# The second FFN's first two blocks on x times A, with the norm's factor and the part of B applied afterwards

## Chip, cores and metric

The kernel runs on one core of one Trainium2 chip. The metric is the device time of one execution in microseconds (us), taken as the median of several runs. Engines are named as in the profile: PE is TensorE's matmuls and PEld its weight loads, DVE is VectorE, ACT is ScalarE, POOL is GpSimd, and SP is SyncE, which issues the DMAs.

## What is computed

The reference is a model block of two layers followed by a second hybrid block. The change touches one place, the feed-forward network (FFN) of the second layer, on the 256 latent tokens (width 1024):

```python
def rmsnorm(x, g):
    y = x * lax.rsqrt(jnp.mean(x * x, axis=-1, keepdims=True) + EPS)
    return y * g

def modulate(x, g, shift, scale):
    return rmsnorm(x, g) * (1 + scale) + shift
...
# FFN: h = modulate(x, ...); u = h @ w_up (1024 -> 2 * 2816);
# a 3x3 depthwise convolution over a grid of 4 rows x 64 tokens, plus a bias;
# hidden = first half * silu(second half); x += gate * (hidden @ w_down)
```

In the kernel's terms h = (x · r) · A + B. A = g · (1 + scale) and B = shift have one value per feature. r is the norm's factor, one value per token.

## The kernel before

Activations lie feature-major: 128 features on the partitions, tokens along the free axis, 8 groups k of 128 features. `xT` is the residual stream in float32; the latent tokens are its columns 256 to 511. Every matmul operand is a pair of a float16 part and a bfloat16 rest (`whi`, `wlo` for weights, `hh`, `hl` for h), and a product takes three passes, whi·hh, whi·hl and wlo·hh (`proj_fm`, line 332).

Layer 1's mixer ends in `ssd`. Its last generator, `out(3, factor)`, multiplies the products `so` by a factor (DVE) and adds them to `xT` (`add_residual`, DVE). Then `ffn(1, ...)` runs:

- `norm_h` (line 378) calls `rstd_bc` (line 354). ACT squares each of the 8 groups and DVE adds them up (`sq`). A matmul with ones gives the sum per token (`ssq`). DVE makes the reciprocal root in eleven small instructions, spreads it on a diagonal (`dg`), and a matmul brings it to all partitions in PSUM (`rbc`, one buffer of the pool `nb`). Then for each k: DVE forms `nt` = x·A·r, ACT rounds it with B to `hh`, DVE forms the rest `hl`.
- The up projection has 22 blocks. Block i has 256 columns of `w_up`, as two channels of 128 (c = 0, 1). For each channel PE makes 8 × 3 matmuls of 256 tokens into a PSUM tile `up` (pool `mm`, 7 buffers). `conv` then has ACT write u = up · w4 + bias, and DVE adds the 8 other taps, each one `scalar_tensor_tensor` (line 1005, recorded at the helper's line 303) that reads `up` from PSUM and `u` from SBUF. ACT takes the silu (`sg`), POOL multiplies (`sg` by u), ACT and POOL split the result into `hidh` and `hidl`.
- The weights of blocks 0 and 1 (`first_up`) are loaded and split during the mixer. Those of block 2 are split by ACT (`whi`) and DVE (`wlo`), those of later blocks by ACT and POOL (`wlo`, 128x2048). The split weights have three buffers, so `whi` of block i waits for PE to be through with block i − 3.
- The down projection (`dn`) follows, with `before_norm` and early weights of the next stage between its steps.

The order on each engine's queue is settled when the program is built: an instruction that is ready goes ahead of an earlier one that still waits, and among ready ones the earlier one in the program goes first. `reuse_waits="tile"` means that a pool's new memory waits for the tiles that lay there before.

Of the kernel before, what the change touches and what calls it, by code (L numbers as in the profile page):

```python
# [10 lines left out]
F32 = mybir.dt.float32  # L11
F16 = mybir.dt.float16
BF16 = mybir.dt.bfloat16
I32 = mybir.dt.int32
U32 = mybir.dt.uint32
AF = mybir.ActivationFunctionType
ALU = mybir.AluOpType
# [231 lines left out]
class Program:  # L249
# [723 lines left out]
    def ffn(self, l, streams):  # L973
        I, V = self.I, self.V
        both = len(streams) == 2
        n, t0 = (512, 0) if both else (256, 256)
        lat = n - 256
        fcb = self.pp("fcb").rearrange("p (l c) -> p l c", l=2)[:, l]
        h = self.h
        if both:  # L980

            self.norm_stream(l, 1, 1)
            first = []
            for i in range(3):
                w = self.get_w(I["w_up"][l, i], 8, 256, self.G)
                first.append((w, [self.mm("up") for _ in range(2)]))
                for c in range(2):
                    self.proj_fm(first[i][1][c][:, :256], w, c * 128, 128, h, 0, 256)
        else:
            self.norm_h(self.xT, t0, n, self.segs(l, 1, streams), h)  # L990

        def conv(u, ps, c):
            w = lambda j: fcw[:, c, j:j + 1]
            self.act(u[:, :n], ps[:, :n], AF.Identity, bias=fcb[:, c:c + 1], scale=w(4))
            if both:
                self.stt(u[:, 1:256], ps[:, 0:255], w(3), u[:, 1:256], ALU.mult, ALU.add)
                self.stt(u[:, 0:255], ps[:, 1:256], w(5), u[:, 0:255], ALU.mult, ALU.add)
            ug, pg = [a[:, lat:lat + 256].rearrange("p (r c) -> p r c", r=4) for a in (u, ps)]
            for dy in (-1, 0, 1):
                for dx in (-1, 0, 1):  # L1000
                    if dy == 0 and dx == 0:
                        continue
                    r0, r1, c0, c1 = max(0, -dy), 4 - max(0, dy), max(0, -dx), 64 - max(0, dx)
                    o = ug[:, r0:r1, c0:c1]
                    self.stt(o, pg[:, r0 + dy:r1 + dy, c0 + dx:c1 + dx], w(3 * dy + dx + 4), o, ALU.mult, ALU.add)

        with ExitStack() as ph:
            fp = self.pool("fp", 1, None, ph)
            f2 = self.pool("f2", 3, None, ph)
            stage = self.pool("stage", 1 if both else 3, None, ph)  # L1010
            fcw = fp.tile([128, 44, 9], F32, name="fcw")
            self.nc.sync.dma_start(fcw, I["fcw"][l].rearrange("p (c j) -> p c j", c=44))
            hid = self.pair(fp, "hid", [128, 22, n])
            if both:
                ms, mp = self.pool("ms", 3, None, ph), self.pool("mp", 3, None, ph)
                up = True
                mods = chain.from_iterable(self.mod_steps(1, r, eng=lambda: self.G if up else None, pool=ms, parts=mp,
                                                          halves=True) for r in range(6))
            for i in range(22):
                begun = both and i < 3  # L1020
                if begun:
                    w, pss = first[i]
                elif not both and i < 2:
                    w = self.first_up[i]
                else:
                    w = self.get_w(I["w_up"][l, i], 8, 256, self.G if both or i > 2 else None, (None, stage)[i % 2])
                us = []
                for c in range(2):
                    ps = pss[c] if begun else self.mm("up")
                    a = 256 if begun else 0  # L1030
                    self.proj_fm(ps[:, a:n], w, c * 128, 128, h, a, n)
                    u = f2.tile([128, n], F32, tag=f"u{c}", name="u")
                    conv(u, ps, 22 * c + i)
                    us.append(u)
                sg = f2.tile([128, n], F32, tag="sg", name="sg")
                self.act(sg[:, :n], us[1][:, :n], AF.Silu)
                self.tt(sg[:, :n], sg[:, :n], us[0][:, :n], ALU.mult, eng=self.G)
                self.split(hid[0][:, i], hid[1][:, i], sg[:, :n], eng=self.G)
                if both:
                    next(mods)  # L1040

            def down(k, ws, a, b):
                ps = self.mm("dn")
                for j, w in enumerate(ws):
                    self.proj_fm(ps[:, a:b], w, 0, 128, hid, a, b, nk=11, h0=11 * j, first=j == 0, last=j == 1)
                    for _ in range(3 - j if both else 0):
                        next(mods, None)
                return ps

            def weights(k, j, parts=None):  # L1050
                return self.get_w(I["w_dn"][l, 2 * k + j], 11, 128, self.G if not both and k < 2 else None, (None, stage)[j], parts)

            up = False
            if not both:
                self.ahead()
            for k in range(6 if both else 8):
                self.add_residual(down(k, [weights(k, j) for j in range(2)], 0, n), l, 5, k, streams, t0)
                if not both:
                    self.before_norm(k)
                    if k >= 4 and k < 4 + 3:  # L1060
                        for i in (0, 1):
                            self.first_mg.append(self.get_w(I["w2_m"][2 * (k - 4) + i], 8, 128, self.G, stage, self.nx, 2048, 1024))
            if both:

                ws = [[weights(k, j, fp if (k, j) == (7, 1) else None) for j in range(2)] for k in (6, 7)]
                for s, a, b in streams:
                    for k in (6, 7):
                        ps = down(k, ws[k - 6], a, b)
                        self.add_residual(ps[:, a:b], l, 5, k, ((s, 0, 256),), a)
                    if s == 0:  # L1070
                        self.norm_stream(1, 0, 0)


    def layer1_mixer(self):
        h, I = self.h, self.I
        self.fu_stack = self.ctx.enter_context(ExitStack())
        with ExitStack() as ph:
            self.fu = self.pool("fu", 2, None, self.fu_stack)
            sp = self.pool("sp", 1, None, ph)
            s2 = self.pool("s2", 2, None, ph)  # L1080

            y = self.pair(sp, "ys", [128, 8, 256])
            self.ssd(sp, s2, h, y)
            self.dbg("ys", y[0])
        self.dbg("xmid1", self.xT[:, :, 256:512])

    def ssd(self, sp, s2, h, y):
# [198 lines left out]
        def heads(g, D):  # L1286
# [3 lines left out]
            for j in range(4):  # L1290
# [41 lines left out]
                                 start=True, stop=True)  # L1332
                self.tt(yt[:, j], yt[:, j], Y[:, :256], ALU.add)
                self.tt(yt[:, j], yt[:, j], D["sz"][:, j], ALU.mult)
                sq = s2.tile([128, 256], F32, tag="ssq", name="ssq", bufs=3)
                self.act(sq, yt[:, j], AF.Square)
                if j:
                    self.tt(sq, sq, sums, ALU.add)
# [663 lines left out]
```

## Time and profile before

| what | us |
|---|---|
| median of 3 runs (range) | 1651.38 (1649.72 to 1652.54) |
| the profiled execution | 1646.42 |
| its span | 1644.6 |
| PE busy in the span | 1563.6 (95%) |
| DVE busy | 1212.3 (74%) |
| ACT busy | 847.9 (52%) |
| POOL busy | 444.8 (27%) |

The span is the profiled execution between its first and last recorded instruction; positions such as 1075.31 are us from its start. Consecutive instructions of one engine overlap in the records, so the spacing of a run of them (its length divided by their count) is what one costs its engine, and it is less than one's recorded duration. A DVE or POOL instruction that is held up after it has been issued appears with a longer duration, not with idle time ahead of it.

### The profile page before, as it was taken

To read this page: it belongs to the slowest core of one execution; us is meant where nothing else is said; L and a number is where in the kernel's file an instruction comes from. 1 tells how busy PE (TensorE), PEld (TensorE's weight loads), DVE (VectorE), ACT (ScalarE), POOL (GpSimd) and SP (SyncE) were. 2 spreads that over 40 slices of the span, in tenths; PEclk is the share of its full clock that TensorE was granted. 3 is DMA by queue.
4 is the path that set the end of the run, shared out by engine and by line. 5 is a ranking of instruction groups with operands and counts; after the bars stand their busy time and mean duration, and the time that the engine had idled before them with its cause. 6 is when DMAs were issued, how large, how long until landed. Compare 5 with 4: busy or idle time off the path is not lost.

```text
span 1644.6 us, 31809 instructions
## 1 busy us (share of the span) xinstructions
PE 1563.6 (95%) x12978; PEld 1083.6 (66%) x12978; DVE 1212.3 (74%) x2637; ACT 847.9 (52%) x1390; POOL 444.8 (27%) x264
## 2 busy tenths in 40 slices
PE   6999999889999999998999999699998999999998
PEld 3565875467444444475566667488887887778877
DVE  6888856777877796557878898799977885366734
ACT  4746434334555445435555665356564644566542
POOL 0000000224878740000000000259934312431250
PEclk9999999989999999999999999799999999999999
DMA  9222135752444437532222343335454343433651
GB/s 392 89 103 79 54 126 208 258 183 80 157 149 146 138 122 254 177 120 77 103 78 95 112 141 125 124 121 199 137 194 166 141 167 111 146 116 125 228 168 52
DMA packets 41187, 236.77 MB, mean 144 GB/s; under 512 B 4689, under 2 KB 5457, under 8 KB 21201
## 3 DMA queue, kind: packets, MB, share of 16 engines
q1 hardware_dynamic: 41040, 234.74, 40.6%
q8 instruction: 102, 1.67, 0.4%
q14 instruction: 45, 0.36, 0.1%
HBM read 233.68 MB, written 1.05 MB: 143 GB/s over the span
## 4 chain that ended last, share of the span: by engine, by line
PE 81%; DVE 8%; ACT 4%; DMA 3%; issue 3%; POOL 1%; ACTq 0%; SPq 0%; DVEq 0%; POOLq 0%
PE up L332 19%; PE dn L332 9%; PE sx L332 5%; PE fm L332 4%; PE mg L332 4%; PE br L332 3%; PE mqk L332 2%; PE tm L339 2%; ACT whi L306 2%; PE so L332 2%; DVE wlo L294 2%; PE mod L505 2%; PE sz L332 2%; DVE u L303 2%; PE sc L1664 2%
## 5 line engine op out<-in xcount | busy, mean ns | idle before, releaser
L332 PEld LDWEIGHTS <-whi 128*128 128x128 f16 (+2 forms) x5240 | 511.5, 99 | 253.3 <-issue 38.1
L294 POOL TENSOR_TENSOR wlo<-st,whi 128x2048 bf16<-128x2048 f32 (+2 forms) x101 | 311.7, 3097 | 935.5 <-ACT whi L306 934.8
L306 ACT ACTIVATE whi<-st 128x2048 f16<-128x2048 f32 (+3 forms) x242 | 369.1, 1536 | 253.3 <-PE dn L332 46.6
L332 PEld LDWEIGHTS <-wlo 128*128 128x128 bf16 (+2 forms) x2620 | 258.9, 99 | 127.4 <-issue 13.6
L294 DVE TENSOR_TENSOR wlo<-st,whi 128x2048 bf16<-128x2048 f32 (+4 forms) x141 | 279.0, 1988 | 83.8 <-ACT whi L306 82.1
L303 DVE SCALAR_TENSOR_TENSOR u<-up,fcw,u 128x189 f32<-128x189 f32 (+3 forms) x792 | 297.3, 431 | 49.4 <-ACT u L306 41.5
L332 PE MATMUL up<-hh,whi 128*128 128x256 f16 (+1 forms) x752 | 238.2, 319 | 4.4 <-ACT hh L306 4.1
L332 PE MATMUL up<-hl,whi 128*128 128x256 bf16 (+1 forms) x752 | 238.1, 317 | 2.0 <-DVE hl L303 1.9
L332 PE MATMUL up<-hh,wlo 128*128 128x256 f16 (+1 forms) x752 | 237.7, 317 | 0.0
L332 PE MATMUL dn<-hidh,wlo 128*128 128x256 f16 (+1 forms) x396 | 122.2, 310 | 2.3 <-DVE wlo L294 2.3
L332 PE MATMUL dn<-hidh,whi 128*128 128x256 f16 (+1 forms) x396 | 122.3, 311 | 1.8 <-ACT whi L306 1.8
L332 PE MATMUL dn<-hidl,whi 128*128 128x256 bf16 (+1 forms) x396 | 122.5, 310 | 0.0
L306 ACT ACTIVATE u<-up,ppt,fcw 128x512 f32<-128x512 f32 (+1 forms) x88 | 58.1, 660 | 47.9 <-PE up L332 47.9
L332 PE MATMUL fm<-hh,whi 128*128 128x256 f16 x288 | 78.5, 273 | 0.5 <-DVE xc L303 0.5
L332 PE MATMUL fm<-hh,wlo 128*128 128x256 f16 x288 | 78.6, 273 | 0.0
L332 PE MATMUL fm<-hl,whi 128*128 128x256 bf16 x288 | 78.5, 273 | 0.0
L332 PE MATMUL mg<-hh,wlo 128*128 128x256 f16 x256 | 71.0, 277 | 3.6 <-POOL wlo L294 3.6
L332 PE MATMUL mg<-hl,whi 128*128 128x256 bf16 x256 | 71.0, 278 | 1.2 <-DVE hl L303 1.2
L332 PE MATMUL mg<-hh,whi 128*128 128x256 f16 x256 | 70.7, 277 | 0.9 <-ACT mgt L306 0.9
L339 PEld LDWEIGHTS <-hh 128*128 128x128 f16 x640 | 61.5, 99 | 8.8 <-issue 1.1
L298 POOL TENSOR_SCALAR E<-E,rs 128x128 f32<-128x128 f32 (+1 forms) x48 | 37.1, 786 | 107.3 <-DVE rs L1675 47.9
L294 POOL TENSOR_TENSOR sg<-sg,u 128x512 f32<-128x512 f32 (+1 forms) x44 | 44.2, 1004 | 45.6 <-ACT sg L306 45.3
(539 smaller groups left out, 3050.8 us busy)
## 6 DMA issues: line engine op xcount, KB each, us to landing
st<-in_w_up_dram SPq DMA_DIRECT2D x44, 1024.0 KB, 4.8
st<-in_w_dram SPq DMA_DIRECT2D x25, 1024.0 KB, 4.9
st<-in_mod_w_dram SPq DMA_DIRECT2D x48, 512.0 KB, 4.7
st<-in_w_dn_dram SPq DMA_DIRECT2D x32, 704.0 KB, 4.1
st<-in_ssd_w_dram SPq DMA_DIRECT2D x20, 1024.0 KB, 4.9
st<-in_mod_w_dram SPq DMA_DIRECT2D x16, 1024.0 KB, 6.4
st<-in_w_m_dram SPq DMA_DIRECT2D x32, 512.0 KB, 4.3
st<-in_even_w_dram SPq DMA_DIRECT2D x14, 1024.0 KB, 5.0
```

Source lines behind the costliest of these rows:

```text
L294: (eng or self.V).tensor_tensor(o, a, b, op=op)
L298: (eng or self.V).tensor_scalar(o, a, s1, None, op0=op0)
L303: self.V.scalar_tensor_tensor(o, a, s, b, op0=op0, op1=op1)
L306: self.S.activation(o, i, func, **kw)
L332: self.T.matmul(ps, w[a][:, k, c0:c0 + cw], h[b][:, h0 + k, t0:t1], start=first and k == 0 and i == 0, stop=last and k == nk - 1 and i == 2)
L339: self.T.matmul(ps, h[b][:, k, t0:t0 + 128], w[a][:, k, c0:c0 + cw], start=k == 0 and i == 0, stop=k == nk - 1 and i == 2)
L505: T.matmul(ps[32 * j:32 * j + 32, :256], c[:, 2 * b + k], w[:, 0 if halves else k, 256 * j:256 * j + 256], start=b == k == i == 0, stop=b ...
L1664: T.matmul(ps[:, a:b], q[r, tb * 128:tb * 128 + 128], k[r, 0:b - a], start=True, stop=False)
```

## The change

Ahead of `norm_h`, x·A (without r and B) is split into the unused columns 256 to 511 of `h`, for all 8 groups. `rstd_bc` is called by itself. Blocks 0 and 1 are multiplied with x·A into four PSUM tiles. B, split and padded to 32 columns, is multiplied with the same weights into a PSUM tile `uB` (four strips of 32 partitions, two k in each), copied to SBUF as a row and summed over its partitions by a matmul with ones; this gives one value per output feature, `ub`. The factor r is copied from PSUM to SBUF (`rb`). When blocks 0 and 1 come up in the loop, DVE multiplies each of their four products by `rb` into an SBUF tile (tag `sg`, 3 buffers), ACT adds `ub` to it in place, and `conv` reads that SBUF tile where it read PSUM before. Blocks 2 to 21 use the normed h as before. The two tiles of B take 1 KB per partition, which the tag `ssq` gives back (3 buffers become 2).

```diff
         else:
-            self.norm_h(self.xT, t0, n, self.segs(l, 1, streams), h)
+            (_, _, A, B), = self.segs(l, 1, streams)
+            for k in range(8):
+                self.split(h[0][:, k, 256:512], h[1][:, k, 256:512], self.xT[:, k, 256:512], scale=A(k))
+            pb = self.rstd_bc(self.xT, t0, n)
+            hB = [self.fb.tile([128, 8, 32], dt, name=m) for m, dt in (("hBh", F16), ("hBl", BF16))]
+            bB = self.modc[l][:, 3, 1]
+            for t in hB:
+                self.G.memset(t, 0.0)
+            self.act(hB[0][:, :, 0], bB)
+            self.tt(hB[1][:, :, 0], bB, hB[0][:, :, 0], ALU.subtract)
+            first = []
+            for w in self.first_up:
+                pss = [self.mm("up") for _ in range(2)]
+                for c in range(2):
+                    self.proj_fm(pss[c][:, :256], w, c * 128, 128, h, 256, 512)
+                ps = self.mm("uB")
+                for k in range(8):
+                    j = k % 4
+                    for i, (a, b) in enumerate(PASSES):
+                        self.T.matmul(ps[32 * j:32 * j + 32, :256], hB[b][:, k], w[a][:, k],
+                                      start=k < 4 and i == 0, stop=k >= 4 and i == 2)
+                row = self.cols.tile([128, 256], F32, tag="mrow", name="mrow", bufs=1)
+                self.act(row, ps[:, :256])
+                for c in range(2):
+                    self.T.matmul(ps[:, 256 + c:257 + c], row[:, c * 128:c * 128 + 128], self.ones[:, 0:1], start=True, stop=True)
+                ub = self.cols.tile([128, 2], F32, tag="ub", name="ub")
+                self.act(ub, ps[:, 256:258])
+                first.append((pss, ub))
+            rb = self.nrm.tile([128, 512], F32, tag="s2", name="rb")
+            self.act(rb[:, :n], pb[:, :n])
+            self.norm_h(self.xT, t0, n, self.segs(l, 1, streams), h, pb)
...
-                    w = self.first_up[i]
+                    pss, ub = first[i]
...
-                    ps = pss[c] if begun else self.mm("up")
-                    a = 256 if begun else 0
-                    self.proj_fm(ps[:, a:n], w, c * 128, 128, h, a, n)
+                    if not both and i < 2:
+                        ps = f2.tile([128, n], F32, tag="sg", name="up")
+                        self.tt(ps, pss[c][:, :n], rb[:, :n], ALU.mult)
+                        self.act(ps, ps, AF.Identity, bias=ub[:, c:c + 1])
+                    else:
+                        ps = pss[c] if begun else self.mm("up")
+                        a = 256 if begun else 0
+                        self.proj_fm(ps[:, a:n], w, c * 128, 128, h, a, n)
...
-            self.fu = self.pool("fu", 2, None, self.fu_stack)
+            self.fu, self.fb = self.pool("fu", 2, None, self.fu_stack), self.pool("fb", 1, None, self.fu_stack)
...
-                sq = s2.tile([128, 256], F32, tag="ssq", name="ssq", bufs=3)
+                sq = s2.tile([128, 256], F32, tag="ssq", name="ssq")
```

## Rows read from the trace of the kernel before

**Rows 1.** Stretches: length, busy (count) of PE, PEld, DVE, ACT, POOL, clock, DMA, GB/s.
```profile
1050.00:1054.50 4.50, 1.36 (x13) 0.97 (x11) 3.85 (x9) 1.63 (x4) 0.00 (x0) 1.00 0.33 67
1054.50:1062.00 7.50, 1.77 (x6) 1.17 (x7) 3.25 (x15) 3.91 (x3) 1.92 (x1) 0.61 0.93 391
...
1110.00:1197.00 87.00, 86.73 (x792) 77.03 (x790) 86.51 (x252) 54.40 (x78) 84.37 (x50) 1.00 0.51 173
```
**Rows 2.** The chain that ended last, from 1073 to 1202: start, us, what.
```profile
1073.31 84.23 PE up L332 x770
...
1172.16 9.52 DVE u L303 x28
...
1184.52 17.58 PE dn L332 x160
```
**Rows 3.** Timeline of DVE from 1053 on: start, us, instruction, [idle before <-releaser].
```profile
1053.43 0.95 DVE L294 TENSOR_TENSOR sq<-sq,s 128x256 f32<-128x256 f32 x2
...
1057.51 0.43 DVE L294 TENSOR_TENSOR dg<-ept,r 128x256 f32<-128x256 f32 x1
...
1059.31 0.87 DVE L303 SCALAR_TENSOR_TENSOR nt<-xT,modA,rbc 128x256 f32<-128x256 f32 x2 [1.38 <-PE rbc L375]
...
1062.23 6.39 DVE L303 SCALAR_TENSOR_TENSOR hl<-nt,modc,hh 128x256 bf16<-128x256 f32 x2 [2.05 <-ACT hh L306]
...
1073.29 0.88 DVE L303 SCALAR_TENSOR_TENSOR hl<-nt,modc,hh 128x256 bf16<-128x256 f32 x2 [0.18 <-ACT hh L306]
1075.31 21.43 DVE L303 SCALAR_TENSOR_TENSOR u<-up,fcw,u 128x189 f32<-128x189 f32 x62 [1.13 <-ACT u L306]
1096.97 23.39 DVE L303 SCALAR_TENSOR_TENSOR u<-up,fcw,u 128x189 f32<-128x189 f32 x69 [0.24 <-ACT u L306]
```
**Rows 4.** Timelines of POOL and DVE, the weight splits beside the norm and after it.
```profile
1060.08 8.27 POOL L294 TENSOR_TENSOR wlo<-st,whi 128x2048 bf16<-128x2048 f32 x2 [437.08 <-ACT whi L306]
...
1064.11 4.24 POOL L294 TENSOR_TENSOR wlo<-st,whi 128x2048 bf16<-128x2048 f32 x1
...
1064.35 4.28 DVE L303 SCALAR_TENSOR_TENSOR hl<-nt,modc,hh 128x256 bf16<-128x256 f32 x1
...
1086.62 4.08 POOL L294 TENSOR_TENSOR wlo<-st,whi 128x2048 bf16<-128x2048 f32 x1 [1.07 <-ACT whi L306]
```
**Rows 5.** Timelines of SP and ACT, the weights of blocks 3 to 5 and the norm.
```profile
1053.31 15.39 SPq L315 DMA_DIRECT2D st<-in_w_up_dram  x5
...
1058.09 3.71 ACT L306 ACTIVATE whi<-st 128x2048 f16<-128x2048 f32 x2 [4.30 <-DMA st<-in_w_up_dram]
...
1061.71 0.89 ACT L306 ACTIVATE hh<-nt,modc 128x256 f16<-128x256 f32 x2
...
1084.64 1.89 ACT L306 ACTIVATE whi<-st 128x2048 f16<-128x2048 f32 x1
```
**Rows 6.** Groups from 1110 to 1197: shapes, xcount | busy us, mean ns | idle before.
```profile
L294 POOL TENSOR_TENSOR wlo<-st,whi 128x2048 bf16<-128x2048 f32 x13 | 53.1, 4082 | 0.0
L303 DVE SCALAR_TENSOR_TENSOR u<-up,fcw,u 128x189 f32<-128x189 f32 x126 | 46.7, 404 | 0.3
```
**Rows 7.** Timelines of DVE and POOL at the end of the down projection.
```profile
1252.06 3.96 DVE L294 TENSOR_TENSOR sq<-sq,s 128x512 f32<-128x512 f32 x1 [1.81 <-ACT s L306]
1255.94 2.34 DVE L303 SCALAR_TENSOR_TENSOR hl<-xT,fg,hh 128x256 bf16<-128x256 f32 x1
...
1251.40 6.60 POOL L294 TENSOR_TENSOR wlo<-st,whi 128x2048 bf16<-128x2048 f32 x2 [12.58 <-ACT whi L306]
```
**Rows 8.** Timeline, nearest instructions to the new ones: split's rest, multiply from PSUM, strip matmuls.
```profile
1208.20 0.48 DVE L303 SCALAR_TENSOR_TENSOR hl<-xT,fg,hh 128x256 bf16<-128x256 f32 x1
...
1034.21 0.42 DVE L294 TENSOR_TENSOR yt<-yt,Y 128x256 f32<-128x256 f32 x1
...
694.75 0.29 PE L505 MATMUL mod<-whi,c 128*32 128x256 f16 x4
694.87 0.28 PE L505 MATMUL mod<-wlo,c 128*32 128x256 bf16 x4
```

## The prediction

> **What bounds the kernel now.** I read the windows first, to find which engine is full around the change, then the chain of waits, to see whose work the end hangs on, then the timelines of DVE, POOL and ACT, to see what ends each wait.
>
> Two stretches matter. While the norm is made, from 1054.5 to 1062, PE works 1.77 us out of 7.5, at a mean granted clock of 0.61 of full speed [rows 1]: it waits for h. In the up projection three engines are full together: from 1110 to 1197 PE is busy 86.73 us of 87, DVE 86.51 and POOL 84.37 [rows 1]. Which of the three sets the pace decides what the change is worth. PE makes 792 matmuls in 87 us, 0.110 each, so a block of 48 takes 5.3 us. DVE's taps come at 21.43 / 62 = 0.346 us [rows 3], so a block of 16 takes 5.5 us: DVE is the slower one. The chain agrees. It follows PE for 84.23 us from 1073.31, but its last stretch before `dn`, from 1172.16, is 9.52 us of taps, and then `dn` [rows 2]: by then PE waits for DVE to free PSUM. DVE's taps begin at 1075.31, are already running without a gap at 1096.97 [rows 3] and have 0.3 us of idle time ahead of 126 of them in the later window [rows 6]. So the end of the up projection is the start of the taps plus DVE's work, and the change has to be judged on DVE.
>
> What fills DVE before 1075.31? The sums end at 1054.4, `dg` at 1057.9, `nt` begins at 1059.31, and the norm ends at 1074.17 [rows 3]. The first two `hl`, alike in shape to the last two, take 6.39 us where the last two take 0.88. They stand beside two weight splits of POOL from 1060.08 to 1068.35: the second `hl` starts at 1064.35 and lasts 4.28 us, as POOL's second split lasts from 1064.11 for 4.24 [rows 4]. The end of the down projection shows the same: a `sq` of 3.96 us and an `hl` of 2.34 beside 6.60 us of POOL splits [rows 7]. So a DVE instruction that reads two SBUF tensors stands still while POOL's split runs. The taps do not: they read `up` from PSUM, and take 404 ns with POOL full beside them [rows 6].
>
> **The change part by part.**
>
> *Split of x·A, 8 `hh` and 8 `hl`.* ACT has room. An `hl` is recorded with 0.48 us [rows 8] and costs about 0.40 in a row. DVE is busy 3.85 us of the 4.5 before the sums are through [rows 1], so 8 × 0.40 = 3.2 us push the sums from 1054.4 to about 1057.5, and `dg` from 1057.51 to about 1060.6. That is late by half a microsecond: POOL's splits start at 1060.08, fixed by the DMA issued at 1053.31 and by ACT's `whi` at 1058.09 [rows 4, 5]. `dg` reads two SBUF tensors, so it waits for the first split and ends near 1064.6; then `rbc`, two `nt`, and `hl` from 1068.4. In the norm of before two `hl` were through by 1068.6, so the norm ends 2 × 0.40 = 0.8 us later, at 1075.0. If `dg` just makes it, nothing is lost: the `hl` would stand behind POOL anyway. If several of the small instructions are caught too, both splits go by first and the whole norm (16 × 0.43 = 6.9 us and its bubbles) follows 1068.4 plus 1 us: 1077. So 0 to +3, and I take +0.8.
>
> *Blocks 0 and 1 early on PE.* 96 matmuls × 0.110 = 10.5 us move into PE's idle stretch. On PE that is a gain of 10.5. On DVE it removes only the 1.13 us between norm and first tap [rows 3], and the new multiply and add take that place. I count 0; bounds −1.1 and +1.
>
> *The products with B.* 48 strip matmuls. Four on different strips take 0.12 us [rows 8], three passes in a row on one strip may cost a full 0.110 each, so 1.4 to 5.3 us of PE. Their operands are ready long before, and PE idles 5.7 us from 1054.5 to 1062 alone. Cost 0, and 5.3 in the worst case on an engine that is then 10.5 us ahead. The copies of row, `ub` and `rb` are ACT's, which has room as well.
>
> *Four multiplies by r.* DVE, from PSUM, like a 0.42 us row of the same shape [rows 8]: 4 × 0.36 in a row, +1.5. These read one SBUF tensor and aren't held up. ACT's four adds hide between taps of the other channel.
>
> *The taps of blocks 0 and 1.* 32 taps × 0.346 = 11.1 us as before, but now both inputs lie in SBUF. Is POOL running meanwhile? Before, those 32 taps ended at 1075.31 + 11.1 = 1086.4, and POOL's next split began at 1086.62 [rows 4], after `whi` of block 5 at 1084.64 [rows 5], which had waited for PE to finish block 2. Now PE has blocks 0 and 1 behind it and finishes block 2 about 1 us after the norm's last `hl`. `whi` (1.9 us) follows behind ACT's first adds and u, and POOL's split starts 3 to 4 us after the norm, in the middle of block 0's taps. Block 3 releases the next split 5.3 us later and block 4 a third. More can't come: PE then lacks PSUM until taps of block 2 run. Each split holds the taps for up to 4.08 us [rows 6]. Bounds: the nearest row by name, the taps of now, says 0; the rows of `hl` and `sq`, with two inputs in SBUF, say up to 3 × 4.08, with `sg` and `hidl` of block 0 on top 13.6. I take two, 8.2, since two inputs in SBUF is what the delayed rows have in common. Here a page speaks against the change. The Trainium skill, page "SBUF — State Buffer", section "SBUF: two separate sides", says that VectorE and GpSimd share one pair of SBUF ports, that an operation with two SBUF inputs takes it for its whole length against a GpSimd operation that reads SBUF, and that the other blocks fully. By it the taps would belong with `hl`, and the sum is +10.5; by the taps' own rows it would be +2.3. No row shows a tap in that form.
>
> *Memory.* The ring `ssq` of 2: a square waits for the sum two steps back, and one lies a whole head behind the other; cost 0, at most 0.4 for each of 16. The shift by 1 KB can move what the DMA at 1053.31 waits for; ±2. Two small fills on POOL fall where it idles.
>
> **Sum.** +0.8 + 0 + 1.5 + 8.2 = +10.5 on DVE. The up projection ends by that much later. PE is far ahead then, the weights of the down projection come a little sooner relative to it, and I let it win back 1.5: +9. On the profiled execution 1646.42 + 9 = 1655.4; this lies 5.0 below the median of the runs, so the median forecast is 1651.4 + 9 = **1660.4**.
>
> **Rivals.**
>
> *Taps not held up:* either the form doesn't matter or POOL's splits come later, behind `sg` of block 0 in ACT's queue. Then +0.8 + 1.5 − 0 to 1.5: about +2, 1653. For it: no tap in this kernel was ever slow. It decides at whether POOL's split starts within 13 us of the norm's end. 0.20.
>
> *PE was the bound, so faster:* the chain gives PE 84 us [rows 2]. If DVE could keep up, the 10.5 us taken from PE's start would show in full, less 1.5: 1642. Against it: DVE's idle time is 0.3 us [rows 6] and PE waits for it at the end. It decides at a DVE gap in the up stage. A split of POOL that moves out of the norm's way (up to 6 us) would help in the same direction. 0.11.
>
> *Caught twice:* several of the root's instructions behind both splits, and three splits with `sg` and `hidl` in the taps: 3 + 1.5 + 13.6 = 18, 1669. 0.13.
>
> **Numbers.** My forecast, +5 to +14 for one to three splits, gets 0.56. Within 0.2% (3.3 us, about what can be told from no change) lies most of the first rival and little of the forecast: 0.19. Faster by more: 0.11. Slower: 0.70. The range leaves out the faster case and the upper part of "caught twice": 1650 to 1668.5.
>
> **What would show it.** After the change: `so` followed by `up` on PE without the idle time and with the clock at 1.00; sums that end near 1057.5; `dg` or a root instruction recorded with several us; taps of the SBUF form with some 4 us each wherever a POOL split of 4.08 runs beside them, two or three of these; block 1's last tap near 1097 where it was 1086.4; taps from PSUM unchanged, DVE full to the end of the up projection. I am wrong if the SBUF taps take 0.4 us beside a POOL split, if POOL's split of block 5 starts after them, or if PE's lead shortens a stage in which DVE shows gaps.

## The result, and the profile after

The changed kernel takes **1662.78 us** (median of 6 runs, 1661.63 to 1671.38) against 1650.55 (6 runs, 1646.36 to 1656.29) for the kernel before, measured beside it: a ratio of 1.0082 with an interval of 1.0054 to 1.011, which is +12.2 us in the medians and 9 to 18 by the interval. The prediction was +9 and 1660.4. The profiled execution took 1661.81 us, its span is 1660.0: 15.4 more than the span before. A profile is one execution, and its total can lie 10 us off the median of its kernel, so the pieces below are compared by the spacing of starts within each profile.

First the windows of the changed kernel (length, then busy time and count of PE, PEld, DVE, ACT and POOL, clock, DMA share, GB/s).

```profile
1050.00:1054.50 4.50, 4.50 (x42) 4.02 (x42) 4.50 (x11) 2.93 (x8) 0.00 (x0) 1.00 0.01 4
1054.50:1062.00 7.50, 7.50 (x70) 5.87 (x71) 6.05 (x17) 3.04 (x8) 0.00 (x0) 1.00 0.42 128
...
1068.00:1085.00 17.00, 13.99 (x126) 11.54 (x125) 16.50 (x36) 6.92 (x17) 5.48 (x2) 0.90 0.37 126
1085.00:1110.00 25.00, 12.96 (x93) 10.14 (x91) 22.29 (x33) 10.81 (x14) 14.10 (x5) 0.77 0.38 127
1110.00:1197.00 87.00, 82.06 (x725) 71.92 (x723) 86.03 (x253) 53.63 (x80) 78.00 (x46) 0.97 0.42 142
```

PE does start early: from 1054.5 to 1062 it is busy all 7.50 us at clock 1.00, where it had 1.77 us at 0.61 [rows 1]; positions in the two profiles can't be laid over each other exactly, since the first `so` comes 4.05 us later now, but the same 7.5 us counted from that `so` are full too. Thirty microseconds later the gain is gone: from 1085 to 1110 PE works 12.96 us of 25 (before, the same 25 us counted from the first `so` were full), and DVE finishes only 33 instructions there. The timeline of DVE shows why.

```profile
1049.26 1.29 DVE L294 TENSOR_TENSOR so<-so,factor 128x512 f32<-128x512 f32 x2 [3.04 <-ACT factor L306]
...
1060.00 0.43 DVE L294 TENSOR_TENSOR sq<-sq,s 128x256 f32<-128x256 f32 x1
...
1064.24 0.42 DVE L294 TENSOR_TENSOR dg<-ept,r 128x256 f32<-128x256 f32 x1
1068.43 0.87 DVE L303 SCALAR_TENSOR_TENSOR nt<-xT,modA,rbc 128x256 f32<-128x256 f32 x2 [3.77 <-ACT rb L306]
1069.21 0.75 DVE L294 TENSOR_TENSOR up<-up,rb 128x256 f32<-128x256 f32 x2
1069.88 4.28 DVE L303 SCALAR_TENSOR_TENSOR hl<-nt,modc,hh 128x256 bf16<-128x256 f32 x2
...
1076.36 0.41 DVE L303 SCALAR_TENSOR_TENSOR u<-up,fcw,u 128x189 f32<-128x189 f32 x1
...
1083.36 0.48 DVE L303 SCALAR_TENSOR_TENSOR hl<-nt,modc,hh 128x256 bf16<-128x256 f32 x1
1083.76 0.87 DVE L303 SCALAR_TENSOR_TENSOR u<-up,fcw,u 128x192 f32<-128x192 f32 x2
1084.54 0.75 DVE L294 TENSOR_TENSOR up<-up,rb 128x256 f32<-128x256 f32 x2
1087.74 0.42 DVE L303 SCALAR_TENSOR_TENSOR u<-up,fcw,u 128x189 f32<-128x189 f32 x1 [2.45 <-ACT u L306]
```

Read from the top: the mixer's factor comes 4.05 us later than before (its first `so` was at 1045.21). The last `sq` ends at 1060.43, `dg` starts at 1064.24, `nt` at 1068.43 after a wait of 3.77 (it was 1.38 [rows 3]). Then taps of block 0 stand between the steps of the norm, one to three in each gap, 0.41 to 0.47 us each: they read SBUF, and POOL is idle there, from 1073.49 to 1086.49. Block 0 is through at 1084.63. Then DVE waits 2.45 us for ACT, and block 1 begins at 1087.74. Its taps, in the summary of the tile `u` from 1085 to 1104.5 (duration in ns: least, median, most; first and last start):

```profile
L303 DVE SCALAR_TENSOR_TENSOR u<-up,fcw,u x16: 394/416/4202, 1087.7 to 1104.4; 128x189 f32<-128x189 f32 x9, 128x252 f32<-128x252 f32 x4, 128x192 f32<-128x192 f32 x3
```

POOL's splits in the timeline of the same kernel:

```profile
1065.38 8.11 POOL L294 TENSOR_TENSOR wlo<-st,whi 128x2048 bf16<-128x2048 f32 x2 [331.00 <-ACT whi L306]
...
1090.56 12.70 POOL L294 TENSOR_TENSOR wlo<-st,whi 128x2048 bf16<-128x2048 f32 x3 [1.13 <-ACT whi L306]
```

Sixteen taps take from 1087.74 to 1104.8, 17.0 us, where sixteen took 5.5 before. The median is 416 ns, so the loss lies in a few: three splits of POOL run back to back from 1090.56 to 1103.26, and each of them holds one tap until it is over (3.89, 3.83 and 4.20 us). Two views cut at other places show the long ones:

```profile
1090.54 5.06 DVE L303 SCALAR_TENSOR_TENSOR u<-up,fcw,u 128x252 f32<-128x252 f32 x4
...
1095.13 8.34 DVE L303 SCALAR_TENSOR_TENSOR u<-up,fcw,u 128x252 f32<-128x252 f32 x3
```

Four taps in 5.06 us hold one of about 4; three in 8.34 hold two. The chain that ended last says the same (start, us, what):

```profile
1088.41 7.26 DVE u L303 x10
1095.67 3.60 issue
1099.27 15.42 DVE u L303 x34
...
1177.16 26.27 PE up L332 x239
```

The taps of block 1 are the path. Beside them PE stands for want of a free PSUM tile, which only taps can free, and once for a split of POOL. Its waits from 1085 to 1115 (us in total, times, longest):

```profile
PE up L332 <- DVE u L303: 10.7, 2, 8.5
PE up L332 <- POOL wlo L294: 3.5, 1, 3.5
```

**Where 15.4 us come from**, each piece as a difference of starts in the two profiles: 1.3 lie ahead of the mixer, in code that both kernels share; 2.7 in the mixer (from layer 0's last `xT` to the first `so`: 311.25 before, 313.97 after); 13.1 between the first `so` and the last tap (152.5 to 165.6); and 1.8 are won back after it. The 13.1 fall into +2.0 (sums), +0.7 (to `dg`), +2.4 (`dg` to `nt`), −5.4 (`nt` to block 0's last tap: 21.6 to 16.2), +0.7 (block 1's multiplies), +2.45 (the wait for ACT), +11.5 (block 1's taps), and −1.2 in blocks 2 to 21.

### The profile page after: what moved, and what is told of

Its sections match the earlier page's. It is cut to its first block, busy times and chain, and to the rows that moved or that the text cites. A ratio compares the mean times of both kernels' runs of the same rounds, so it can differ in the third digit from the quotient of the medians.

```text
span 1660.0 us, 31886 instructions
## 1 busy us (share of the span) xinstructions
PE 1564.4 (94%) x12968; PEld 1085.7 (65%) x13034; DVE 1223.7 (74%) x2650; ACT 852.3 (51%) x1408; POOL 446.7 (27%) x266
## 4 chain that ended last, share of the span: by engine, by line
PE 77%; DVE 12%; issue 3%; ACT 3%; DMA 3%; POOL 1%; SPq 0%; ACTq 0%; DVEq 0%; POOLq 0%
PE up L332 18%; PE dn L332 8%; PE sx L332 5%; DVE u L303 5%; PE fm L332 4%; PE mg L332 3%; PE br L332 3%; PE mqk L332 2%; DVE wlo L294 2%; PE so L332 2%; ACT whi L306 2%; PE mod L505 2%; PE sz L332 2%; PE tm L339 2%; PE sc L1700 2%
## 5 line engine op out<-in xcount | busy, mean ns | idle before, releaser
L303 DVE SCALAR_TENSOR_TENSOR u<-up,fcw,u 128x189 f32<-128x189 f32 (+3 forms) x792 | 309.7, 447 | 51.3 <-ACT u L306 43.4
L332 PE MATMUL up<-hh,whi 128*128 128x256 f16 (+1 forms) x752 | 238.4, 321 | 13.5 <-DVE u L303 13.5
L332 PE MATMUL up<-hl,whi 128*128 128x256 bf16 (+1 forms) x733 | 233.4, 320 | 3.0 <-DVE hl L303 3.0
L332 PE MATMUL dn<-hidl,whi 128*128 128x256 bf16 (+1 forms) x384 | 117.0, 306 | 0.0
```

Source lines behind the costliest of these rows:

```text
L303: self.V.scalar_tensor_tensor(o, a, s, b, op0=op0, op1=op1)
L332: self.T.matmul(ps, w[a][:, k, c0:c0 + cw], h[b][:, h0 + k, t0:t1], start=first and k == 0 and i == 0, stop=last and k == nk - 1 and i == 2)
```

## The experiments

All ratios are to the kernel before, run beside the experiment on the same chip; the kernel before had a median of 1648.91 us (23 runs) beside four of them (taps from PSUM, the pair at another place, the smaller ring, B written late) and 1648.08 (29 or 35 runs) beside the others. Positions in different traces are compared from the first `so` of each.

**Taps from PSUM.** The multiply and the add stay in place in PSUM, so the taps of blocks 0 and 1 read PSUM as all others do; nothing else changes.

```diff
-                        ps = f2.tile([128, n], F32, tag="sg", name="up")
-                        self.tt(ps, pss[c][:, :n], rb[:, :n], ALU.mult)
-                        self.act(ps, ps, AF.Identity, bias=ub[:, c:c + 1])
+                        ps = pss[c]
+                        self.tt(ps[:, :n], ps[:, :n], rb[:, :n], ALU.mult)
+                        self.act(ps[:, :n], ps[:, :n], AF.Identity, bias=ub[:, c:c + 1])
```

> The changed kernel, but the multiply by r and the add of ub are made in place in PSUM, so the 32 taps of blocks 0 and 1 read PSUM again; everything early stays early. Theory (POOL's weight splits hold taps whose two inputs lie in SBUF): block 1's taps, 17.1 us in the changed kernel, come back to some 5.5 to 6 us with three splits beside them, and the time falls by about 11 us, to 1652. Rival 1 (the early products keep six PSUM buffers and PE starves of PSUM): these buffers are now held longer, not shorter, so the time stays at 1662 or rises. Rival 2 (the order of work in the mixer is the whole loss): 1662.

Measured: 1651.48 us, ratio 1.0028 [1.0005, 1.0051], so 9 us of the 13.5 that the ratio of the change stands for are gone (11 in the medians). The taps from 1080 to 1112 in the tile's summary of this run:

```profile
L303 DVE SCALAR_TENSOR_TENSOR u<-up,fcw,u x79: 391/403/469, 1080.7 to 1111.7; 128x189 f32<-128x189 f32 x39, 128x192 f32<-128x192 f32 x20, 128x252 f32<-128x252 f32 x20
```

Two of POOL's splits beside them, in its timeline:

```profile
1096.18 4.09 POOL L294 TENSOR_TENSOR wlo<-st,whi 128x2048 bf16<-128x2048 f32 x1 [16.49 <-ACT whi L306]
1101.60 4.10 POOL L294 TENSOR_TENSOR wlo<-st,whi 128x2048 bf16<-128x2048 f32 x1
```

Of 79 taps the longest is 0.469 us. The ones beside these two splits belong to blocks 2 and 3, which read PSUM in every kernel. Block 1's last tap ended at 1095.94, 40.6 us after the first `so` where it was 55.5 in the change, and so just ahead of the first split: this run shows what the SBUF tiles cost, but no tap of block 1 had to pass a split. In the second of the two tries below seven of them do, from PSUM (the tile's summary, and POOL's timeline beside it):

```profile
L303 DVE SCALAR_TENSOR_TENSOR u<-up,fcw,u x7: 402/468/468, 1086.3 to 1088.4; 128x252 f32<-128x252 f32 x4, 128x189 f32<-128x189 f32 x3
...
1086.26 4.08 POOL L294 TENSOR_TENSOR wlo<-st,whi 128x2048 bf16<-128x2048 f32 x1 [1.13 <-ACT whi L306]
```

Beside a split a tap takes at most 0.47 us with one input in PSUM, and with both in SBUF the change has one held for 3.83 to 4.20 by each split.

**The other side of the same pair.** The taps keep reading SBUF as in the change, and the splits of blocks 5 to 7 go from POOL to DVE.

```diff
-  self.G if both or i > 2 else None
+  self.G if both or i > 7 or i in (3, 4) else None
```

> The changed kernel with the weight splits of blocks 5 to 7 on DVE where POOL did them; the taps of blocks 0 and 1 read SBUF as in the change. Theory (a tap with both inputs in SBUF is held only while POOL runs a split): the taps of block 1 come at 0.35 us each, 11.5 us less than in the changed kernel, and DVE gets 3 splits of about 2.3 us, 6.9 more: about 1658, a ratio to the kernel before of 1.004 to 1.007. Rival (the SBUF form is slow by itself, or waits for ACT's add): taps as long as in the changed kernel and 6.9 us more: about 1669, 1.012.

Measured: 1658.49 us, 1.0064 [1.0042, 1.0085], where 1.004 to 1.007 was expected. The taps from 1076 to 1101 in the tile's summary:

```profile
L303 DVE SCALAR_TENSOR_TENSOR u<-up,fcw,u x34: 397/406/901, 1076.8 to 1100.7; 128x189 f32<-128x189 f32 x18, 128x192 f32<-128x192 f32 x8, 128x252 f32<-128x252 f32 x8
```

The first of DVE's three splits, in its timeline:

```profile
1093.29 2.27 DVE L294 TENSOR_TENSOR wlo<-st,whi 128x2048 bf16<-128x2048 f32 x1
```

Without a split on POOL the SBUF form costs what the PSUM form costs, 406 ns against 403; the longest, 0.901, stands beside a POOL `hidl` of 0.67. So it is neither the form by itself nor POOL by itself, but both at a time. The Trainium skill's page "SBUF — State Buffer", section "SBUF: two separate sides", has this as a lock that one of the two holds for its whole instruction when DVE has two SBUF inputs; the taps of 3.83 to 4.20 us beside splits of 4.16 to 4.37 agree, and so do those of 0.40 to 0.47 from PSUM.

**The pair at another place.** The kernel before, with an ACT copy of `up` to SBUF ahead of the taps of blocks 8 and 9, in the middle of the up projection, where POOL is full.

```diff
+                    if not both and i in (8, 9):
+                        sb = f2.tile([128, n], F32, tag="sg", name="up")
+                        self.act(sb, ps[:, :n])
+                        ps = sb
```

> The kernel before, with one thing added: for blocks 8 and 9, in the middle of the up projection where POOL is full, ACT copies the product to an SBUF tile and the 32 taps read that. The suspected cost by itself. Theory: while POOL has a split running these taps stand still, one tap gets through per split, and it goes on until PE has no PSUM left and POOL runs dry; three splits or so, +8 to +14 us, 1659 to 1665, with taps of 4 us. Rival (the form of the taps doesn't matter): four copies of 0.4 us on ACT, which has room; 1650.5 to 1652, taps of 0.4 us.

Measured: 1678.09 us, 1.0178 [1.0153, 1.0202], which is +29 us, more than expected. All 352 taps of this kernel in one line of the tile's summary:

```profile
L303 DVE SCALAR_TENSOR_TENSOR u<-up,fcw,u x352: 394/411/9044, 1080.6 to 1226.4; 128x189 f32<-128x189 f32 x80, 128x192 f32<-128x192 f32 x54, 128x252 f32<-128x252 f32 x42
```

Eight taps of the two blocks, in DVE's timeline:

```profile
1129.82 12.34 DVE L303 SCALAR_TENSOR_TENSOR u<-up,fcw,u 128x189 f32<-128x189 f32 x8 [4.89 <-ACT u L306]
```

POOL's timeline beside them:

```profile
1129.31 4.06 POOL L294 TENSOR_TENSOR wlo<-st,whi 128x2048 bf16<-128x2048 f32 x1
1133.34 1.29 POOL L294 TENSOR_TENSOR hidl<-sg,hidh 128x256 bf16<-128x256 f32 x2
1134.60 4.05 POOL L294 TENSOR_TENSOR wlo<-st,whi 128x2048 bf16<-128x2048 f32 x1
```

One tap lasts 9.04 us: POOL's four instructions from 1129.31 to 1138.65 follow each other without a gap, and the tap outlasts all of them. Two more taps are held, for 4.31 and 4.04 us. With ACT's copies came waits of 4.89, 1.14 and 1.66 us for `u`. The three held taps (16.2 us over a free one's 0.4 each) and the three waits (7.7) add up to 23.9, and DVE's last tap ends 23.8 us later from the first `so` than before. My count had splits alone, one tap each.

**The smaller ring alone.** The kernel before with the tag `ssq` at 2 buffers.

```diff
-                sq = s2.tile([128, 256], F32, tag="ssq", name="ssq", bufs=3)
+                sq = s2.tile([128, 256], F32, tag="ssq", name="ssq")
```

> The kernel before with only the ring ssq cut from 3 to 2 buffers; the order of all queues is the same as before. Theory (the 4 us by which the factor of the mixer comes later are not the ring's): 1650.5, within 0.2%, factor at 1044 to 1046. Rival (the shorter ring makes ACT's squares wait): up to +3, 1653.5, with idle time of ACT's ssq behind DVE's ssq.

Measured: 1649.36 us, 1.000 [0.9982, 1.0018]. The ring costs nothing.

**B written late.** What makes the mixer longer? The order of the queues is settled when the program is built, and B has been ready since layer 0. The write of `hBh` in the tile's summary of the changed kernel:

```profile
L306 ACT ACTIVATE hBh<-modc x1: 238/238/238, 734.2 to 734.2; 128x8 f16<-128x8 f32 x1
```

And in that of the run with both edits, which follows below:

```profile
L303 DVE SCALAR_TENSOR_TENSOR hBh<-xT,modc x1: 191/191/191, 1056.2 to 1056.2; 128x8 f16<-128x8 f32 x1
```

In the change the small write is placed at 734 us, 315 us ahead of its use, and behind it the order on ACT, DVE and PE through the whole mixer is another one than before. The edit ties it to the last token of `xT` (times 0), and the mixer has the order of the kernel before again, instruction for instruction on DVE (495 of them) and ACT (335).

```diff
-            self.act(hB[0][:, :, 0], bB)
+            self.stt(hB[0][:, :, 0], self.xT[:, :, 511], 0.0, bB, ALU.mult, ALU.add)
```

> The changed kernel, but the first write of B's split takes a zero times the last token of x with it, so that it can't be placed before the mixer ends. Theory (the two small instructions of B, which the scheduler puts at the end of layer 0, reshuffle the queues of the whole mixer and cost some 3 us there): the factor comes at 1045 to 1046 where it was at 1048.8, and the time falls by 2.5 to 4, to 1659 to 1660. Rival 1 (the 4 us are scatter between executions or the 1 KB shift): 1662 to 1663. Rival 2 (the order of work is the whole loss and not the taps): 1651.

Measured: 1658.91 us, 1.0067 [1.005, 1.0085]. Block 1's taps stay held, in the tile's summary of this run:

```profile
L303 DVE SCALAR_TENSOR_TENSOR u<-up,fcw,u x44: 399/410/4217, 1073.0 to 1105.9; 128x189 f32<-128x189 f32 x23, 128x192 f32<-128x192 f32 x12, 128x252 f32<-128x252 f32 x9
```

The interval overlaps that of the change, so this time alone doesn't settle it. The length of the mixer does. From layer 0's last `xT` to the first `so` the profiles have 309.6 to 311.3 us in all ten kernels of the old order and 314.0 to 314.1 in all three with B early: 2.7 to 4.5 us. The ten share one order of DVE and ACT there. Which of the moved instructions costs the time I did not trace.

**Both edits.** Taps from PSUM and B late.

> The changed kernel with both earlier edits: multiply and add in place in PSUM, and B's first write tied to the last token of xT. Theory (the time of the change is the taps held by POOL's splits plus the new order in the mixer, and PE's early start is worth nothing while DVE is full): 1662.8 - 11 - 4 = about 1648, a ratio to the kernel before of 0.997 to 1.002. Rival (DVE is not the bound once its taps run freely, so the 10.5 us that PE starts early come through): about 1640, a ratio of 0.994 or less. The two edits do not add (both end at the same wait): about 1652, 1.002 or more.

Measured: 1644.27 us, 0.9982 [0.9958, 1.0006]: 3 us under the kernel before, which can't be told from no change. With it the four corners are known:

| ratio to the kernel before | taps of blocks 0, 1 from SBUF | from PSUM |
|---|---|---|
| B early | 1.0082 (the change) | 1.0028 |
| B late | 1.0067 | 0.9982 |

At 1650 us, the taps' side is worth 0.0054 and 0.0085 (9 and 14 us), B's time 0.0015 and 0.0046 (2 and 8); with the intervals of the four ratios, neither pair of values can be told apart. The traces are sharper: from the first `so` to the first `xT` of the down projection they have 171.1 and 156.3 us in the upper row, 170.3 and 156.1 in the lower, and 157.2 before, so the taps' side is 14.8 and 14.2, and B's time lies ahead of the first `so`. What remains of the change, 10.5 us of PE's work done early at the price of eight rests and four multiplies on DVE, nets next to nothing. The up projection of this kernel in the windows:

```profile
1110.00:1197.00 87.00, 85.43 (x777) 75.65 (x775) 87.00 (x256) 53.96 (x81) 85.16 (x52) 1.00 0.50 173
```

DVE is busy 87.00 of 87. From the first `so` its last tap ends after 151.4 us; before, 152.5.

**40 taps less, in the kernel before.** If DVE sets the pace, how close behind is the next engine?

```diff
-                    if dy == 0 and dx == 0:
+                    if dy == 0 and dx == 0 or not both and few and dy and dx > 0:
```

> The kernel before, with 40 of the second FFN's 352 taps left out (the two taps to the right, above and below, in both channels of blocks 6 to 15); the output lacks them. DVE has 40 x 0.346 = 13.8 us less to do in the middle of the up projection. Theory (DVE sets the pace, PE is close behind at 5.3 us a block against 5.5): the time falls, but only until PE, which began with the normed h, is full without a wait: by 3 to 7 us, 0.996 to 0.998. Rival (PE sets the pace already): no change, 0.999 to 1.001. Rival (DVE alone, PE has much in hand): 13 us less, 0.992.

Measured: 1644.89 us, 0.9974 [0.9953, 0.9995]: of 13.8 us taken from DVE 4 come through (0.8 to 7.8 by the interval), as the first theory said. The window from 1110 to 1190:

```profile
1110.00:1190.00 80.00, 80.00 (x735) 71.71 (x734) 76.04 (x209) 52.44 (x77) 80.00 (x48) 1.00 0.51 174
```

PE and POOL are now both at 80.00 of 80.

**40 taps less, with PE's early start.** The same taps left out of the run with both edits.

> The run with both edits (multiply and add in PSUM, B's first write late), with the same 40 taps left out. Theory (PE's early start is real and lies behind DVE): here PE is 10.5 us ahead, so all of the 13.8 us that DVE loses come through: 11 to 14 us below the run with both edits and some 6 to 9 us below the kernel before with 40 taps less; a ratio to the kernel before of 0.991 to 0.993. Rival (PE's early start is lost again before the middle of the up projection, or is worth nothing for another reason): the same as the kernel before with 40 taps less, 0.996 to 0.998.

Measured: 1644.08 us, 0.9974 [0.9947, 1.0002], the same as without the early start. My theory fell: I had taken the 10.5 us for time that lies behind DVE. From the first `so` to the first `xT` of the down projection this run takes 152.4 us and the one without the early start 153.2. The trace shows where the time goes. After the first two blocks PE needs the normed h, and DVE now makes it with the taps of block 0 in between; the last `hl` ends 38.0 us after the first `so`, where it was 29.2 in the kernel before with 40 taps less. PE's waits from 1068 to 1110 (us in total, times, longest):

```profile
PE up L332 <- DVE hl L303: 5.8, 5, 2.6
```

And POOL, the last pair of numbers ahead of the clock, has become the full engine. The up projection of this run in the windows, and below it that of the kernel before with 40 taps less:

```profile
1088.00:1198.00 110.00, 109.44 (x1002) 97.61 (x1001) 100.03 (x280) 70.14 (x105) 110.00 (x65) 1.00 0.51 173
1089.00:1199.00 110.00, 110.00 (x1011) 98.59 (x1009) 101.99 (x281) 70.26 (x103) 108.74 (x64) 1.00 0.50 172
```

From its split of block 5 to its last `hidl` POOL is not idle at all here, and this split comes 40.9 us after the first `so`, hardly sooner than the 41.6 without the early start: its `whi` waits for PE to be through with block 2, which needs the normed h.

**The norm first.** So I forbade the taps between: `rb` is written from the norm's last rest (times 0) and `rbc`, again with 40 taps less.

```diff
-            self.act(rb[:, :n], pb[:, :n])
             self.norm_h(self.xT, t0, n, self.segs(l, 1, streams), h, pb)
+            self.stt(rb[:, :n], h[1][:, 7, :n], 0.0, pb[:, :n], ALU.mult, ALU.add)
```

> The run with both edits and 40 taps less, with rb written by DVE from the last rest of the norm (times 0) and rbc, so that no multiply or tap of blocks 0 and 1 can stand between the steps of the norm; the 40 taps are left out as before. Where the taps stood between, the last hl of the norm ended 38.0 us after the factor of the mixer, in the kernel before with 40 taps less 29.2. Theory (PE's head start of 10.5 us was handed back there, since PE waits for the normed h of block 2): the last hl ends about 31 us after the factor, PE goes on with block 2 some 7 us sooner, and the time falls by 4 to 7 us against the run with both edits and 40 taps less: a ratio to the kernel before of 0.993 to 0.995. Rival (POOL, busy 80.00 us of 80 in the up projection of both runs with 40 taps less, sets the pace whatever PE does): no change, 0.997 to 0.998.

Measured: 1653.9 us, 1.0017 [0.9994, 1.004], by the ratios 7 us more than without the edit; both theories fell. The norm did end sooner, 30.4 us after the first `so`, as wanted. But PE's waits in the same window became these:

```profile
PE up L332 <- DVE u L303: 9.8, 2, 5.0
PE up L332 <- DVE hl L303: 2.7, 1, 2.7
```

Now the taps start later, at 1078.63, and PE stands for want of a free `up` tile: with the four products of blocks 0 and 1 waiting for their taps, three of the seven tiles are left. PE can lead DVE by seven tiles and no more, whichever order DVE takes. POOL's split of block 5 did come 6.3 us sooner, but POOL was then idle for 9.7 us, which it was not without this edit:

```profile
1080.50:1199.00 118.50, 110.87 (x983) 97.81 (x984) 110.06 (x308) 73.30 (x111) 108.83 (x65) 0.96 0.46 156
```

The first `xT` of the down projection comes 3.7 us later from the first `so` than without this edit. That covers the 2.5 us by which the two profiled executions differ; where the other 3 us of the medians' loss arise I did not settle.

**Two tries at a faster kernel**, from the run with both edits. In the first the call of the norm moves behind block 0, so that taps from PSUM can run while POOL's splits hold the `hl`. In the second, block 1's products also wait for `rb`, so that `rbc` does not stand behind them on PE.

```diff
+                if not both and i == 1:
+                    self.norm_h(self.xT, t0, n, self.segs(l, 1, streams), h, pb)
...
+                if first:
+                    rb = self.nrm.tile([128, 512], F32, tag="s2", name="rb")
+                    self.act(rb[:, :n], pb[:, :n])
+                    for p in pss:
+                        self.T.matmul(p[:, 0:1], self.ones, rb[:, 0:1], start=True, stop=True)
```

> The run with both edits (multiply and add in PSUM, B's first write late), with the call of the norm moved behind block 0 in the program, so that block 0's multiplies and taps go first where both are ready. Theory (DVE sets the pace; what is to be won is its time beside POOL's two splits, in which an hl stands still and a tap from PSUM does not): 1 to 3 us less than the run with both edits, a ratio to the kernel before of 0.996 to 0.998. Rival (the hl are held as before, or ACT's add and u come too late for the taps to fill the gap): the same, 0.998 to 1.000.

> As the run with the norm behind block 0, and block 1's products made to wait for rb (a one-column matmul that reads rb goes first into each of its PSUM tiles), so that rbc does not stand behind them in PE's queue. Theory (the wait for rb of 3.77 us ahead of the norm, against 1.38 in the kernel before, is time of the path): 2.4 us less than the run with only the norm moved, a ratio to the kernel before of 0.994 to 0.997. Rival (the norm then only runs into POOL's splits sooner, and both end as late): no change against that run.

Measured: 1647.34 us, 0.9982 [0.9957, 1.0008], and 1646.08 us, 0.9982 [0.996, 1.0005]: both the same as the run with both edits, and none of the three can be told from the kernel before. In the second the wait only moved. Its timeline of PE:

```profile
1061.79 0.76 PE L375 MATMUL rbc<-dg,ones 128*128 128x256 f32 x2 [2.07 <-DVE dg L294]
```

And its timeline of ACT:

```profile
1060.39 3.71 ACT L306 ACTIVATE whi<-st 128x2048 f16<-128x2048 f32 x2 [3.63 <-DMA st<-in_w_up_dram]
1064.00 0.36 ACT L306 ACTIVATE mrow<-uB 128x256 f32<-128x256 f32 x1
1064.27 0.37 ACT L306 ACTIVATE rb<-rbc 128x256 f32<-128x256 f32 x1
```

`rbc` follows `dg` at once, at 1061.79, and its copy `rb` then waits for ACT's two `whi` until 1064.27. Whatever is freed on one queue meets the weights of blocks 3 and 4 on another.

## Why the prediction was right, and where its terms were not

The size was right to 3 us, +9 against +12.2, and that is partly luck: the norm's first `nt` came 5.1 us later where +0.8 stood, and taps that ran within the norm won back 5.4, which stood nowhere. By its own steps:

- **What bounds the kernel.** DVE, with PE and POOL close behind: shown. Taking 13.8 us from DVE gives 4 us; giving PE 10.5 us gives 3 or nothing. With 40 taps less it is POOL that has no idle time left.
- **Splits of x·A, +0.8.** The sums came 2.0 us later, not 3.2. `dg` was not caught by POOL: the splits started at 1065.38, 5.3 us later than before, 4.05 of which came with the later first `so`, and `dg` at 1064.24 was ahead of them. Instead of that, `rbc`, whose `dg` was done at 1064.66, stood on PE behind block 1's products until 1067.38 and `nt` with it, +2.4. I had put the early products down at no cost to DVE because PE idles there; that PE works in order, and that a matmul which the norm needs stands behind them, was missing.
- **What took it back.** The held pair of `hl` took 4.28 us, not 6.39, and the taps of block 0 filled the gaps in which the norm waits for ACT: −5.4. From the first `so` to block 0's last tap the two kernels differ by −0.3 us. None of these pieces was in the sum as it came.
- **Four multiplies, +1.5.** Pairs of 0.75 us, so 1.3 to 1.5: right.
- **The taps, +8.2.** The mechanism was right, in both directions of it (taps from PSUM pass a split, SBUF taps without POOL are free). The size was too small: +11.5, three splits and not two, inside the bounds of 0 to 13.6. My place for it was wrong too. Block 0 escaped, since its taps ran within the norm; all three splits met block 1, because DVE got one tap through for each, and so the taps were still there when the next split came.
- **A wait that was not in the sum, +2.45.** I let ACT's adds hide between taps of the other channel. These rows of ACT in the changed kernel show what they stood behind:

```profile
1084.70 1.28 ACT L306 ACT_TABLE_LOAD   x1 [2.09 <-DVE u L303]
1085.99 0.42 ACT L306 ACTIVATE sg<-u 128x256 f32<-128x256 f32 x1
1086.32 0.89 ACT L306 ACTIVATE up<-up,ub 128x256 f32<-128x256 f32 x2
1087.12 1.26 ACT L306 ACTIVATE u<-up,ppt,fcw 128x256 f32<-128x256 f32 x2
```

  Block 0's silu needs a table load, and block 1's adds come after both. With the multiply and add in place in PSUM these adds start 25.8 us after the first `so`, here 37.1: block 1's multiplies come only with block 0's last taps, at 1084.54. I read that as the ring of the tag `sg`, of whose three tiles block 0's products hold two until then; it was not tested by itself, but in the run with the taps from PSUM DVE has no such wait.
- **The products with B, 0.** Not quite right for PE: 24 of the strip matmuls stood ahead of `rbc`, with no idle time around them. In the chain that ended last they take 0.32, 0.32 and 0.77 us, so up to 1.4 of the +2.4 above is theirs. And the sentence that their operands are ready long before names what cost 2.7 to 4.5 us: an instruction that is ready early is placed early, and the order of the mixer changed with it.
- **Memory, 0.** Right, by the run with the smaller ring. The shift of the weights' DMA showed no cost of its own, and I did not test it alone.
- **Won back in the down projection, −1.5.** 1.8.

The forecast's DVE sum, +10.5, stands against +13.1 from the first `so` to the last tap, and a term of about 3 us for the mixer was missing; the 1.3 us ahead of the mixer lie in shared code, and I count them as scatter. The rival "taps not held up" (+2) falls by the taps of 3.83 to 4.20 us, "PE was the bound" by the run with both edits. "Caught twice" had three splits right, and the root's instructions wrong: none of them was held.

## What to carry to other kernels

Before an operand is moved from PSUM to SBUF, look at what POOL does in that stretch: a DVE instruction with one PSUM input ran beside it for nothing, and one with two SBUF inputs stood still for POOL's whole instruction, time after time. An early start of an engine is worth something only where the next one can follow; here the factor that DVE needs came no sooner, POOL's split of block 5 came hardly sooner, and PE can lead by the seven tiles of its pool. And where a builder orders the queues by readiness, a constant that is written from old data moves far ahead and can change the order of a stage that it has nothing to do with: compare the order of the whole program, or tie the write to late data.

## What the runs showed of the hardware that I had not expected

- POOL's splits and DVE's taps took turns in the change (three splits in 12.70 us, one held tap of 3.83 to 4.20 for each), but not with blocks 8 and 9, where one tap lasted 9.04 us through four POOL instructions. Not every SBUF tap that starts inside a split is held: in the change those at 1090.93 and 1095.13 took 0.47 us.
- The same split takes 2.27 us on DVE and 4.08 to 4.10 on POOL, so moving three of them to DVE cost less than leaving three taps held: 1.0064 against 1.0082, though these two intervals overlap. From the first `so` the last tap ends 4.3 us sooner (161.36 and 165.65).
- A tap with both inputs in SBUF is as fast as one from PSUM when POOL is idle: 406 and 403 ns in the median.
